# Which side of a PSUM-to-SBUF copy takes the step: writes in ascending order and interleaved reads, in place of the reverse

## The chip, the cores and the metric

The kernel runs on one core of one Trainium2 chip. The metric is the device time of one execution in microseconds (us), as the chip reports it. Before the change it was 951.44 us, the median of three runs (950.08 to 952.41).

## The reference

Attention within windows of 64 rows: q, k and v are fp32 of shape (4, 4096, 1536), and each window looks only at itself.

```python
q_w = q.reshape(B, nw, W, D)           # W = 64, nw = 64; k and v likewise
logits = np.einsum('bnwd,bnud->bnwu', q_w, k_w) * D ** -0.5
logits = logits - logits.max(axis=-1, keepdims=True)
attn = np.exp(logits)
attn = attn / attn.sum(axis=-1, keepdims=True)
out = np.einsum('bnwu,bnud->bnwd', attn, v_w)
```

## The kernel before

The 16384 rows are cut into 32 units of 512 rows. For each unit the kernel loads q, k and v from HBM (casting to fp16 on the way), transposes q and k on TensorE, multiplies, takes the exponential, multiplies with v, scales and stores. The transposes move pairs of fp16 as if they were fp32 words. Four transposes of 128x128 go into one of two PSUM buffers of 128x512 fp32, called banks here, and one copy then takes the bank to SBUF, alternately by VectorE (even g) and by ScalarE (odd g), 12 copies a unit. The cut below is shortened, with comments added.

```python
tps = [ps(f"tp{i}", [P, R, H, P]) for i in range(2)]     # two PSUM banks, R = H = 2
...
        for g in range(2 * DC):                  # TensorE; DC = 6; g < DC is q, then k
            transpose(g)                         # waits for the copy of g - 2 (same bank)
            if g >= DC + 2:
                for h in range(H):
                    product(g - DC - 2, h)
...
    def copy_out(eng, copy, g):
        xt = xq if g < DC else xk
        await_(eng, p_t[g % 2])                  # the four transposes of g are done
        if g % DC == DC - 1:
            eng.sem_inc(m_q if g < DC else m_k, 1)   # q16 or k16 may be loaded again
        dst = xt[:, g % DC, :].rearrange("p (r e j) -> p r j e", r=R, j=H)
        copy(out=dst, in_=tps[g % 2][:, :, :, :]).then_inc(f_c[g % 4], 1)
...
        gp.wait_ge(m_q, u + 1)                   # GpSimd issues the transfers
        load("q", u + 1, q16, d_q)
        ...
        gp.wait_ge(m_k, u + 1)
        load("k", u + 1, k16, d_k)
```

DC is 1536 / 256 = 6. The bank holds `r j e`; the products want `r e j` in SBUF. So somewhere the order has to turn. Before, the copy reads PSUM straight through and writes every second fp32 word of SBUF, a step of 8 bytes, then comes back for the words between.

The softmax here doesn't subtract the row's maximum and nothing guards it: scores larger than these inputs give would overflow.

## Time and profile before

| what | before |
|---|---|
| median time | 951.44 us |
| span of the profiled run | 949.5 us |
| bytes over HBM | 302 MB read, 101 MB written |
| busy: PE / VectorE / ScalarE | 609.7 / 278.7 / 331.3 us |
| the changed copies: VectorE / ScalarE | 192 of 692 ns / 192 of 617 ns |
| mean granted TensorE clock (1 is full speed) | 0.855 |

The page has one digit for each fortieth of the span (9 is 90% or more busy) and a list of groups of instructions: line, engine, operation, tiles, count, then the busy us in total, the mean ns of one, and the idle time of that engine in front of them. The lines themselves stand in the prediction. One view more, the list of waits: here is what TensorE's transposes waited for in the kernel before (engine, tile, line, what was waited for, us in total, times, longest us).

```profile
PE tp L148 <- PEq L214: 244.1, 33, 16.7
PE tp L148 <- DVE xq L223: 47.9, 64, 1.0
```

The first line is TensorE standing idle until q or k has been loaded; nearly all of it is the wait for k (224.9 us before the k transposes), 7 to 8 us in most units. The second is TensorE waiting for a copy to free a bank.

### The profile page before, as it was taken

The page shows a single profiled execution, that of the slowest core. Times are in us where ns is not written, and L with a number is a line of the kernel's source. Part 1 is how long each engine was busy: PE and PEld are TensorE (multiplying, and loading weights), DVE is VectorE, ACT ScalarE, POOL GpSimd, SP SyncE. Part 2 cuts the span into 40 slices and gives each one's busy share as a digit, 9 for nine tenths or more (in the row PEclk, how much of TensorE's full clock was granted, in tenths as well). Part 3 has the DMA queues.
Part 4 walks back from the last instruction along what each step waited for, and adds up shares of the span by engine and source line. Part 5 has one row for each costly group of instructions (what it writes and reads, how often), then busy time and mean ns, then how long its engine had stood idle before and what let it go on. Part 6 is the DMA issues. An engine that isn't in the chain of part 4 may idle for free. (4 is left out here: it accounts for less than half of the span.)

```text
span 949.5 us, 11240 instructions
## 1 busy us (share of the span) xinstructions
PE 609.7 (64%) x4096; PEld 393.6 (41%) x3456; DVE 278.7 (29%) x454; ACT 331.3 (35%) x642; POOL 97.4 (10%) x140
## 2 busy tenths in 40 slices
PE   2776855577565776656865558655577565776682
PEld 2544543354433444424544335443344433444450
DVE  1331413332133331333322333223332132331341
ACT  1442513443233432234432344323443233432252
POOL 4230100110001100101001010010110001100010
PEclk9997977997788987889887898787997788987796
DMA  9999999999999999999999999999999999999997
GB/s 249 216 284 283 238 247 282 279 284 267 235 277 281 285 280 238 261 280 283 283 254 245 281 280 284 272 234 272 281 283 281 243 256 281 282 282 261 235 236 300
DMA packets 26938, 253.34 MB, mean 267 GB/s; under 512 B 2096, under 2 KB 2096, under 8 KB 10544
## 3 DMA queue, kind: packets, MB, share of 16 engines
q0 software_dynamic: 26352, 248.52, 99.8%
q1 hardware_dynamic: 576, 4.72, 1.3%
q14 instruction: 8, 0.07, 0.0%
q8 instruction: 2, 0.03, 0.0%
HBM read 301.99 MB, written 100.66 MB: 424 GB/s over the span
## 5 line engine op out<-in xcount | busy, mean ns | idle before, releaser
L148 PE MATMUL tp<-ident,k 128*128 128x128 f32 x768 | 155.1, 349 | 231.4 <-PEq L214 224.9
L148 PEld LDWEIGHTS tp<-ident,k 128*128 128x128 f32 x768 | 120.4, 182 | 252.1 <-issue 249.6
L160 PE MATMUL lt<-xq,xk 128*128 128x256 f16 x1536 | 216.1, 293 | 0.0
L223 ACT COPY xk<-tp 128x512 f32<-128x512 f32 x96 | 59.2, 617 | 417.8 <-ACTq L214 417.8
L223 DVE COPY xk<-tp 128x512 f32<-128x512 f32 x96 | 66.5, 692 | 381.8 <-DVEq L214 381.8
L160 PEld LDWEIGHTS lt<-xq,xk 128*128 128x128 f16 x1536 | 160.1, 104 | 33.2
L148 PE MATMUL tp<-ident,q 128*128 128x128 f32 x768 | 104.0, 280 | 66.6 <-DVE xq L223 47.1
L148 PEld LDWEIGHTS tp<-ident,q 128*128 128x128 f32 x768 | 86.4, 143 | 100.5 <-issue 99.9
L269 ACT ACTIVATE et<-lt,zeros 32x128 f16<-32x128 f32 x256 | 92.0, 360 | 39.4 <-ACTq L214 36.2
L223 ACT COPY xq<-tp 128x512 f32<-128x512 f32 x96 | 59.3, 617 | 107.3 <-ACTq L214 107.3
L116 PE MATMUL o<-v,et 128*128 128x512 f16 x384 | 93.3, 379 | 0.0
L189 PEld LDWEIGHTS <-et 128*128 128x128 f16 x384 | 30.2, 97 | 151.3 <-issue 114.3
L256 DVE TENSOR_SCALAR out<-o,rs 128x512 f32<-128x512 f32 x128 | 90.2, 747 | 7.7
L223 DVE COPY xq<-tp 128x512 f32<-128x512 f32 x96 | 66.1, 689 | 78.0 <-DVEq L214 78.0
L116 PE MATMUL tp<-v,et 128*128 128x512 f16 x256 | 75.8, 377 | 0.0
L109 POOL DMA_DIRECT2D k<-in_k_dram x31 | 17.4, 562 | 416.5 <-ACTq L221 416.3
L246 DVE RECIPROCAL rs<-sp 128x2 f32<-128x2 f32 x64 | 10.6, 166 | 157.8 <-DVEq L214 157.6
L280 ACT ACTIVATE out<-tp,rs 128x512 f32<-128x512 f32 x64 | 44.0, 688 | 35.8 <-ACTq L214 31.3
L256 DVE TENSOR_SCALAR out<-tp,rs 128x512 f32<-128x512 f32 x64 | 48.1, 751 | 26.2 <-DVEq L214 26.2
L116 PE MATMUL lt<-v,et 128*128 128x512 f16 x128 | 48.3, 377 | 0.0
L109 POOL DMA_DIRECT2D v<-in_v_dram x29 | 20.5, 706 | 238.2 <-DVEq L255 238.2
L280 ACT ACTIVATE out<-o,rs 128x512 f32<-128x512 f32 x64 | 44.1, 688 | 0.0
(26 smaller groups left out, 132.6 us busy)
## 6 DMA issues: line engine op xcount, KB each, us to landing
out_dram<-out POOLq DMA_DIRECT2D x31, 3072.0 KB, 28.5
k<-in_k_dram POOLq DMA_DIRECT2D x31, 1536.0 KB, 20.6
q<-in_q_dram POOLq DMA_DIRECT2D x30, 1536.0 KB, 21.6
v<-in_v_dram POOLq DMA_DIRECT2D x29, 1536.0 KB, 18.9
vs<-in_v_dram POOLq DMA_DIRECT2D x2, 1536.0 KB, 29.7
out<-in_q_dram SPq DMA_DIRECT2D x2, 768.0 KB, 6.5
out<-in_q_dram SPq DMA_DIRECT2D x1, 1536.0 KB, 11.5
out<-in_q_dram POOLq DMA_DIRECT2D x1, 1536.0 KB, 22.7
```

The costliest lines, as they stand in the source:

```text
L109: nc.gpsimd.dma_start(out=slots(dst, 0, SLOTS, r), in_=rows(src, u * UR, SLOTS, r)).then_inc(s, 16)
L116: return nc.tensor.add_instruction(mybir.InstMatmult(name=nc.get_next_instruction_name(), engine=PE, ins=[low(rhs), low(w)], outs=[low(o)] ...
L148: ins = nc.tensor.transpose(tps[g % 2][:, r, j, :], pairs[:, c * P : (c + 1) * P], ident[:, :])
L160: ins = nc.tensor.matmul(lts[h][:, r, :, :], lhsT=halves(xk, c)[:, r, h, :, w], rhs=halves(xq, c)[:, :, h, :, w], start=(c == 0 and w == 0 ...
L189: ld = nc.tensor.ldweights(w)
L223: copy(out=dst, in_=tps[g % 2][:, :, :, :]).then_inc(f_c[g % 4], 1)
L246: ve.reciprocal(out=rs[:, n : n + R], in_=sp[:, n : n + R]).then_inc(n_d, 1)
L256: ins = ve.tensor_scalar_mul(scaled(u, n, j), bank(n, j), scalar1=rs[:, n : n + 1])
L269: ins = sc.activation(ets[h][s, :, :, s], lts[h][s, :, :, s], EXP, bias=zeros[s, 0:1], scale=scale)
L280: ins = sc.activation(scaled(u, n, j), bank(n, j), COPY, bias=0.0, scale=rs[:, n : n + 1])
```

## The change

Its intent is to let SBUF be written in ascending order, and to take the turn on the PSUM side: the copy alternates between two places of the bank that lie 512 bytes apart. The same words end up in the same places, and the instructions stay the same in number and order.

```diff
-        dst = xt[:, g % DC, :].rearrange("p (r e j) -> p r j e", r=R, j=H)
-        copy(out=dst, in_=tps[g % 2][:, :, :, :]).then_inc(f_c[g % 4], 1)
+        dst = xt[:, g % DC, :].rearrange("p (r e j) -> p r e j", r=R, j=H)
+        src = tps[g % 2][:, :, :, :].rearrange("p r j e -> p r e j")
+        copy(out=dst, in_=src).then_inc(f_c[g % 4], 1)
```

## The prediction

> **What bounds the kernel now.** I read the page's slices first, then the DMA queues, then the groups, the order of time on the GpSimd queue in mid-run, and last the ending.
>
> The slices show, for each fortieth of the span, busy tenths of an engine.
>
> ```profile
> PE   2776855577565776656865558655577565776682
> DVE  1331413332133331333322333223332132331341
> ACT  1442513443233432234432344323443233432252
> DMA  9999999999999999999999999999999999999997
> q0 software_dynamic: 26352, 248.52, 99.8%
> HBM read 301.99 MB, written 100.66 MB: 424 GB/s over the span
> ```
>
> The DMA row is full from the first slice to the last but one; VectorE and ScalarE are rarely above four tenths. The last line is the bytes that have to move whatever the engines do: 402.65 MB. [...]I take the kernel as DMA bound, and ask only whether the change can open a hole in that full row.
>
> The copies that the change touches are these four groups (line, engine, operation, tiles, count, busy us, mean ns, then the idle time before them). The fifth line is a PSUM reader with unit steps on both sides, as a yardstick.
>
> ```profile
> L223 ACT COPY xk<-tp 128x512 f32<-128x512 f32 x96 | 59.2, 617 | 417.8 <-ACTq L214 417.8
> L223 DVE COPY xk<-tp 128x512 f32<-128x512 f32 x96 | 66.5, 692 | 381.8 <-DVEq L214 381.8
> L223 ACT COPY xq<-tp 128x512 f32<-128x512 f32 x96 | 59.3, 617 | 107.3 <-ACTq L214 107.3
> L223 DVE COPY xq<-tp 128x512 f32<-128x512 f32 x96 | 66.1, 689 | 78.0 <-DVEq L214 78.0
> L256 DVE TENSOR_SCALAR out<-o,rs 128x512 f32<-128x512 f32 x128 | 90.2, 747 | 7.7
> ```
>
> They take 66.1 + 66.5 = 132.6 us of VectorE and 118.5 us of ScalarE, and those engines stand idle in front of them for 459.8 and 525.1 us. That idle time is the room for a slower copy.
>
> The timeline of the GpSimd queue gives when each transfer is issued (start us, us, what, idle before and releaser). First two units in which the data was late, then one in which it was not.
>
> ```profile
> 499.79 0.70 POOL L109 DMA_DIRECT2D v<-in_v_dram  x1 [8.51 <-DVEq L255]
> 504.30 0.56 POOL L109 DMA_DIRECT2D q<-in_q_dram  x1 [3.81 <-ACTq L221]
> 504.86 0.71 POOL L286 DMA_DIRECT2D out_dram<-out  x1
> 520.75 0.56 POOL L109 DMA_DIRECT2D k<-in_k_dram  x1 [15.18 <-ACTq L221]
> 529.82 0.71 POOL L109 DMA_DIRECT2D v<-in_v_dram  x1 [8.51 <-DVEq L255]
> ...
> 87.27 0.56 POOL L109 DMA_DIRECT2D k<-in_k_dram  x1 [17.34 <-ACTq L221]
> ...
> 107.90 0.56 POOL L109 DMA_DIRECT2D k<-in_k_dram  x1 [5.78 <-ACTq L221]
> ```
>
> From v to v is 30.0 us. A unit moves 402.65 / 32 = 12.6 MB, which in that time is 419 GB/s; the mean unit, (886.2 - 100.9) / 27 = 29.1 us between q issues, moves 433 GB/s. The unit from 87.27 to 107.90 is 20.6 us: there k already lay in place, and that is the pace of the compute alone. **So each unit has 29.1 - 20.6 = 8.5 us of slack on the compute side.**
>
> There is a second cushion, the queue itself. The k load issued at 520.75 finds the store of 504.86 in front of it, which takes 28.5 us (the median to landing) and so lands at 533.4: the engines have work for 12.6 us more. A k load could be issued up to some 10 us later without an idle engine.
>
> The ending has no cushion of that sort, so I read it apart (windows: busy us of PE, weight loads, VectorE, ScalarE, GpSimd, then clock, DMA share, GB/s).
>
> ```profile
> 930.00:935.00 5.00, 1.75 (x9) 0.20 (x2) 2.43 (x5) 1.84 (x3) 0.57 (x1) 0.88 1.01 430
> 935.00:940.00 5.00, 0.00 (x0) 0.00 (x0) 0.00 (x0) 0.00 (x0) 0.00 (x0) 0.50 1.01 433
> 940.00:945.00 5.00, 0.00 (x0) 0.00 (x0) 0.00 (x0) 0.00 (x0) 0.00 (x0) 0.50 0.46 197
> ```
>
> The engines finish at 932.9 and the DMA goes on to about 940 + 0.46 x 5 = 942.3. Only stores are left there. The first half of the last store is issued at 931.89; the DMA then has 942.3 - 931.9 = 10.4 us of work, of which the last store's own 3.15 MB takes 7.3 us at 430 GB/s. So 3.1 us of older stores still stand in front of it.
>
> [...]
>
> **The change part by part.** It adds and removes no instruction: the order on every engine is the same, the 384 copies stay, and matmuls read the same layout. No semaphore moves. What changes is the step on either side of the copies.
>
> 1. *Writing SBUF in order.* Nothing is gained[...]: 0 ns a copy.
> 2. *Reading PSUM interleaved.* Either free (692 and 617 ns stay)[...].
> 3. *On the path of one unit*, in the costly case. q transposes run in pairs with one copy on each engine, and each pair's transposes wait for the copies of the pair before (47.1 us in total of PE waiting for VectorE's xq copies). Two such waits lie in the q stage[...]. In the k stage the copies lie beside products; about one wait is exposed[...], and one more where k follows q at once. [...]against 8.5 us of slack: 0 us of the span in units 1 to 30.
> 4. *The start.* Four loads and the stores queue behind each other by then; the first refill, of q, is issued at 44.5, and the loads issued up to 17.5 are 6 x 7.3 = 44 us of work from 7.6 on, so till about 52. A delay of 2 to 3 us fits: 0 us.
> 5. *The ending.* From the k transposes of unit 30 (893.5) there is no more waiting for data except the last v, so the delays add up[...].
>
> Sum: 951.4 + 0 if the read is free[...].
>
> **The rivals.** (a) *The copies get faster and the time with them.* [...]A copy 100 ns faster would give at most 18 x 0.1 = 1.8 us in the ending, and that only if the stores in front were not the bound: 950 to 951. (b) [...]. (c) *The copies are slower, as in step 2, and a release comes so late that DMA idles.* For it: m_k and m_q are given by ScalarE in the order of its copies, so they do move. Against it: 12.6 us of queue in front of k. It would show less than a full DMA row.[...]
>
> **Range and chances.** [...]the middle is 952. The three runs of before spread over 2.3 us,[...] 949.5 to 954.5 for 8 times in 10. More than 2% slower needs 970, which only rival (b) reaches: 2%. More than 2% faster needs 932[...]: under 1%. The rest is within 2%.
>
> **What would show it.** Right: the DMA row still nines, HBM rate 423 to 425 GB/s, the wait of k's issue near 15 us less 1 to 2. Step 1 is wrong if a copy falls below 680 (VectorE) or 605 ns (ScalarE). Step 2 is read off the same four rows: unchanged[...]. Step 3 is wrong if the wait of PE for VectorE's xq copies in total grows by more than 32 x 1.5 us, step 5 if the last store is issued later than 936. The prediction as a whole is wrong if slices with a DMA share under nine appear in mid-run.

The sum came to 951.4 us if the read is free and to 952.9 us if it is not; the 952 lies between. Rival (b): a read so dear that the copies become the bound, at 985 us. An estimate: (b) needs each of the six pairs of a unit to take over 8.5 / 6 = 1.4 us longer before the slack is used up.

## The result, and the profile after

The changed kernel took 952.55 us (median of 4 runs, 952.39 to 952.75) against 951.65 us for the kernel before (4 runs, 950.08 to 952.41). The ratio is 1.0012 with a 95% interval of 0.9994 to 1.0029: the same.

The page of the changed kernel, in the lines that answer to those of before:

```profile
PE   2775755686565776666765567655587565776582
DVE  1331413332233321333322333223332132331341
ACT  1432513443233432244332344223343233432252
DMA  9999999999999999999999999999999999999996
HBM read 301.99 MB, written 100.66 MB: 424 GB/s over the span
...
L224 ACT COPY xk<-tp 128x512 f32<-128x512 f32 x96 | 56.3, 586 | 417.3 <-ACTq L214 417.3
L224 DVE COPY xk<-tp 128x512 f32<-128x512 f32 x96 | 66.4, 692 | 378.8 <-DVEq L214 378.8
L224 ACT COPY xq<-tp 128x512 f32<-128x512 f32 x96 | 56.3, 586 | 113.6 <-ACTq L214 113.6
L224 DVE COPY xq<-tp 128x512 f32<-128x512 f32 x96 | 66.1, 688 | 81.8 <-DVEq L214 81.8
```

The row of DMA is as full as before and HBM runs at the same 424 GB/s. VectorE's copies are what they were (688 to 692 ns). ScalarE's copies are 586 ns in place of 617, and the spread is gone: they ran from 608 to 635 ns before and from 586 to 587 after. So 192 x 31 ns = 6.0 us of ScalarE's work have vanished, and nothing came of it. The unit in mid-run shows why (timeline of the GpSimd queue: start us, us, transfer, idle before and releaser):

```profile
500.58 0.71 POOL L109 DMA_DIRECT2D v<-in_v_dram  x1 [8.51 <-DVEq L256]
...
521.51 0.56 POOL L109 DMA_DIRECT2D k<-in_k_dram  x1 [15.14 <-ACTq L221]
530.57 0.71 POOL L109 DMA_DIRECT2D v<-in_v_dram  x1 [8.51 <-DVEq L256]
```

From v to v is 30.0 us again. In front of k's issue the queue waits 15.14 us in place of 15.18: the transfers set the pace, as before. In the ending, the stretch of time from unit 30's k transposes to the last store's issue was 932.91 - 893.57 = 39.3 us before and is 933.69 - 894.58 = 39.1 us.

### The profile page after: what moved, and what is told of

It is laid out like the page before. It is cut to its first block, busy times and chain, and to the rows that moved or that the text cites. A ratio compares the mean times of both kernels' runs of the same rounds, so it can differ in the third digit from the quotient of the medians.

```text
span 950.7 us, 11240 instructions
## 1 busy us (share of the span) xinstructions
PE 611.6 (64%) x4096; PEld 395.1 (42%) x3456; DVE 278.7 (29%) x454; ACT 325.3 (34%) x642; POOL 97.3 (10%) x140
## 5 line engine op out<-in xcount | busy, mean ns | idle before, releaser
L148 PE MATMUL tp<-ident,k 128*128 128x128 f32 x768 | 155.2, 349 | 227.7 <-PEq L214 220.7
L160 PE MATMUL lt<-xq,xk 128*128 128x256 f16 x1536 | 216.5, 293 | 0.0
L224 ACT COPY xk<-tp 128x512 f32<-128x512 f32 x96 | 56.3, 586 | 417.3 <-ACTq L214 417.3
L148 PE MATMUL tp<-ident,q 128*128 128x128 f32 x768 | 105.5, 282 | 69.1 <-DVE xq L224 46.5
L224 ACT COPY xq<-tp 128x512 f32<-128x512 f32 x96 | 56.3, 586 | 113.6 <-ACTq L214 113.6
L109 POOL DMA_DIRECT2D v<-in_v_dram x29 | 20.4, 705 | 238.2 <-DVEq L256 238.2
```

Of the source, the lines that this page charges most:

```text
L109: nc.gpsimd.dma_start(out=slots(dst, 0, SLOTS, r), in_=rows(src, u * UR, SLOTS, r)).then_inc(s, 16)
L148: ins = nc.tensor.transpose(tps[g % 2][:, r, j, :], pairs[:, c * P : (c + 1) * P], ident[:, :])
L160: ins = nc.tensor.matmul(lts[h][:, r, :, :], lhsT=halves(xk, c)[:, r, h, :, w], rhs=halves(xq, c)[:, :, h, :, w], start=(c == 0 and w == 0 ...
L224: copy(out=dst, in_=src).then_inc(f_c[g % 4], 1)
```

## The experiments

Two questions were open. What does each side of a copy cost, in itself? And is there really no time to be had or lost by a copy in this kernel, or did a gain and a loss cancel? The first four runs answer the first question. The diffs below are shortened: `# q:` and `# k:` stand for the two branches of `if g < DC`, and `.then_inc(...)` is left out where it did not change.

**e_sides: both sides straight, and both sides stepped.** In q copies neither side has a step, in k copies both have. The data comes out scrambled, so the result is wrong.

```diff
+        line = xt[:, g % DC, :]
+        bank_ = tps[g % 2][:, :, :, :].rearrange("p r j e -> p (r j e)")
+        # q:
+        copy(out=line, in_=bank_)
+        # k:
+        copy(out=line.rearrange("p (m j a) -> p a m j", j=2, a=2),
+             in_=bank_.rearrange("p (j a m) -> p a m j", j=2, a=2))
```

> Wrong results on purpose. q copies have unit steps on both sides; k copies have the stepped write of before (8 bytes) and an interleaved read together. Theory (the interleaved read is free, the stepped write costs ScalarE 31 ns): q copies 586 ns on ScalarE and 692 on VectorE, k copies 617 and 692. Rival (the read is what made ScalarE faster, or unit steps on both sides would be faster still): q copies below 570 on ScalarE or below 680 on VectorE, or k copies 586. Time within 0.5% of before.

Groups of copies, with their mean ns after the busy us:

```profile
L227 ACT COPY xk<-tp 128x512 f32<-128x512 f32 x96 | 59.5, 619 | 418.8 <-ACTq L214 418.8
L225 ACT COPY xq<-tp 128x512 f32<-128x512 f32 x96 | 56.3, 586 | 107.7 <-ACTq L214 107.7
L227 DVE COPY xk<-tp 128x512 f32<-128x512 f32 x96 | 66.5, 693 | 382.0 <-DVEq L214 382.0
L225 DVE COPY xq<-tp 128x512 f32<-128x512 f32 x96 | 66.1, 688 | 76.4 <-DVEq L214 76.4
```

A copy with no step at all (586 and 688 ns) is no faster on either engine than the changed one (586, and 688 to 692), so the interleaved read of PSUM cost nothing here. The stepped write alone brings ScalarE's 31 ns (617 before, 619 here), whether or not the read has a step too. The rival falls.

**e_write: longer steps of the write.** Reads are straight; q copies write one word of each 16 bytes; k copies put successive words 512 bytes apart, going round four places. Its output is wrong, which doesn't matter for the time.

```diff
+        # q:
+        copy(out=line.rearrange("p (m a) -> p a m", a=4), in_=bank_.rearrange("p (a m) -> p a m", a=4))
+        # k:
+        copy(out=line.rearrange("p (a m) -> p m a", a=4), in_=bank_.rearrange("p (m a) -> p m a", a=4))
```

> Wrong results on purpose. Reads have unit steps; q copies write with a step of 16 bytes[...], k copies with a step of 512 bytes. Theory[...]: longer than at 8 bytes on ScalarE[...], and on VectorE above 692 for the first time[...]. Rival (the 31 ns are the price of any pattern with a step, whatever its size): 617 on ScalarE and 692 on VectorE for both.

```profile
L225 ACT COPY xq<-tp 128x512 f32<-128x512 f32 x96 | 102.0, 1062 | 109.8 <-ACTq L214 109.8
L227 ACT COPY xk<-tp 128x512 f32<-128x512 f32 x96 | 101.6, 1058 | 339.2 <-ACTq L214 339.2
L225 DVE COPY xq<-tp 128x512 f32<-128x512 f32 x96 | 101.2, 1054 | 80.6 <-DVEq L214 80.6
L227 DVE COPY xk<-tp 128x512 f32<-128x512 f32 x96 | 100.7, 1049 | 316.6 <-DVEq L214 316.6
```

A step of 16 bytes costs VectorE 1054 - 688 = 366 ns and ScalarE 1062 - 586 = 476 ns, and 512 bytes cost no more than 16. So of the two distances the longer one did not count. Why such writes take longer was not shown, and no step between 8 and 16 bytes was tried. A step of 8 bytes cost nothing on VectorE (692 ns either way) and 31 ns on ScalarE. The rival, the same price for any step, falls. And with copies half as long again or more, the single run, of unknown state, took 951.61 us, much as the kernel before.

**e_read: longer steps of the read.** The changed read goes back and forth between only two places; a longer round might have cost more. Here q copies read with a step of 16 bytes, k copies go round four places 512 bytes apart. Writes are straight. Its output is wrong, which doesn't matter for the time.

```diff
+        # q:
+        copy(out=line.rearrange("p (a m) -> p a m", a=4), in_=bank_.rearrange("p (m a) -> p a m", a=4))
+        # k:
+        copy(out=line.rearrange("p (m a) -> p m a", a=4), in_=bank_.rearrange("p (a m) -> p m a", a=4))
```

> Wrong results on purpose. Writes have unit steps; q copies read PSUM with a step of 16 bytes, k copies round robin over four places 512 bytes apart. The changed kernel's read alternates between two places only[...]. Theory (a read of PSUM by these engines costs the same in any order): 586 ns on ScalarE and 692 on VectorE for both. Rival[...]: the 16-byte step or the four places, or both, show more[...].

```profile
L227 DVE COPY xk<-tp 128x512 f32<-128x512 f32 x96 | 66.4, 692 | 380.4 <-DVEq L214 380.4
L227 ACT COPY xk<-tp 128x512 f32<-128x512 f32 x96 | 56.3, 587 | 419.1 <-ACTq L214 419.1
L225 ACT COPY xq<-tp 128x512 f32<-128x512 f32 x96 | 56.3, 586 | 110.3 <-ACTq L214 110.3
```

VectorE's q copies were 688. In all the patterns tried, straight, between two places, with a step of 16 bytes and round four places, the copies took 688 to 692 ns on VectorE and 586 to 587 on ScalarE.

**e_split: fixed cost or rate.** Every copy is done in two halves of 256 columns, q in the form of before, k in the form of after. The result is right.

```diff
+        for r in range(R):
+            ins = copy(out=..., in_=...)       # the half r, in the one form or the other
+        ins.then_inc(f_c[g % 4], 1)
```

> Right results. Every copy is done in two halves of 256 columns, q with the stepped write of before, k with the interleaved read of after. It tells whether ScalarE's 31 ns are a fixed cost of an instruction or a rate. Theory (a rate: 0.06 ns for each element written with a step): [...]16 apart. Rival (fixed): halves 31 apart[...].[...]

```profile
L226 ACT COPY xq<-tp 128x256 f32<-128x256 f32 x192 | 64.0, 389 | 110.2 <-ACTq L214 110.2
L232 ACT COPY xk<-tp 128x256 f32<-128x256 f32 x192 | 62.1, 375 | 408.6 <-ACTq L214 408.6
```

The halves are 14 ns apart, close to half of 31: ScalarE's cost went with the number of words written, 31 / 512 = some 0.06 ns each. With the copies of 512 there are now two lengths for each form. With the step, (617 - 389) / 256 = 0.89 ns a word over a fixed 161 ns; without it, (586 - 375) / 256 = 0.82 ns a word over a fixed 164. VectorE's halves took 419 and 420 ns, (688 - 419) / 256 and (692 - 420) / 256 = 1.05 to 1.06 ns a word, so much the same in both forms.

**t_null and t_after: is the 0.9 us between the medians real?** The first result left a difference of 0.1%. The kernel before and the changed one were both timed again, five rounds, on one chip, with no edit.

> The kernel before, unaltered, timed against itself: it shows how small a difference these rounds can tell. Theory (the 0.9 us between the medians of after and before are scatter of the transfers): ratio 1.000 with an interval of about 0.2% either way, and single runs that spread over 2 us as before. Rival (the kernel before is steady and after is really 1 us slower): runs of this kernel stay within 0.5 us of each other around 951.4.

> The changed kernel, unaltered, in the same rounds as the null. Theory: ratio 0.999 to 1.002, with one among the intervals covering 1; copies 692 ns on VectorE and 586 on ScalarE again. Rival (the change costs about 1 us, by some way yet to be found): ratio 1.001 with an interval that excludes 1, in rounds in which the null includes it.

The null gave 951.53 us (950.96 to 952.78), ratio 0.9998, interval 0.9985 to 1.0012. The changed kernel gave 951.91 us (950.66 to 953.59), ratio 1.0001, interval 0.9988 to 1.0015; the kernel before in these rounds had 951.91 us (9 runs). The 0.9 us did not come back, and an effect of more than about 0.15% either way is excluded. That is all that can be said: a tenth of a microsecond could not be seen here.

**e_eight: longer copies, in pieces.** Each copy of the changed kernel is cut in eight pieces of 64 elements, which needs no added semaphore. A copy then takes 1.14 us on VectorE and 1.03 on ScalarE in the timeline, against 0.69 and 0.59. The result is right.

```diff
-        copy(out=dst, in_=src).then_inc(f_c[g % 4], 1)
+        for r in range(R):
+            for e in range(0, P, P // 4):
+                ins = copy(out=dst[:, r, e : e + P // 4, :], in_=src[:, r, e : e + P // 4, :])
+        ins.then_inc(f_c[g % 4], 1)
```

> Right results. The changed kernel with every copy in eight pieces of 64 elements[...]. Theory (8.5 us of compute slack in each unit, and a backlog of stores at the end): the time grows by 0 to 2 us, 951 to 954. Rival (slower copies delay the releases, and DMA idles): [...]1010 or more.

It took 952.58 us (4 runs, 951.95 to 953.34) against 951.59 us; ratio 1.0008, interval 0.9991 to 1.0025. The theory holds, the rival of 1010 us falls. The waits of TensorE in this run show where the longer copies went:

```profile
PE tp L148 <- PEq L214: 178.1, 29, 16.7
PE tp L148 <- DVE xq L226: 80.3, 68, 1.5
PE tp L148 <- DVE xk L226: 19.7, 32, 1.0
```

The wait for loaded data shrank from 242.9 us in the changed kernel to 178.1, by 65 us or 2.1 us a unit. The waits for copies grew from 49.6 to 100.3 us, by 51 us or 1.6 us a unit; the busy time of TensorE's groups grew as well, by 21 us (q transposes 105.5 to 119.9, k transposes 155.2 to 156.9, products 216.5 to 221.5), at a mean clock of 0.819 in place of 0.857. Slack was turned into waiting for copies and into slower matmuls, and the transfers noticed nothing. Only in the ending is there no slack: from unit 30's k transposes to the last store's issue took 936.74 - 894.85 = 41.9 us, 2.8 more than in the changed kernel. The windows show that the backlog of stores then just ran out (five us each; the last two numbers are DMA share and GB/s):

```profile
935.00:940.00 5.00, 0.58 (x3) 0.00 (x0) 1.61 (x3) 1.30 (x3) 0.57 (x1) 0.79 0.90 375
940.00:945.00 5.00, 0.00 (x0) 0.00 (x0) 0.00 (x0) 0.00 (x0) 0.00 (x0) 0.50 0.86 361
```

The share of 0.90 is a hole of half a microsecond. In the changed kernel the second of these windows has a share of 0.64, so the transfers ended about (0.86 - 0.64) x 5 = 1.1 us later here: of the 2.8 us, 1.1 showed.

**e_thirtytwo: copies long enough to use up the slack.** The same with 32 pieces of 16 elements (`P // 16` in place of `P // 4`). The result is right.

> Right results. The changed kernel with every copy in 32 pieces of 16 elements[...]. Theory: the unit's compute grows[...] from 20.6 to about 32, which is more than the 29.1 of its transfers: the slack is used up and the time is 1000 to 1070. Rival (the slack is larger than I read it): under 970.

It took 1141.98 us, ratio 1.1998 (1.1978 to 1.2018). A copy took 260.3 / 96 = 2.7 us on VectorE and 244.5 / 96 = 2.5 on ScalarE (busy time of the q copies). Copies do become the bound, so the slack is finite, as the theory has it. But the size is missed: from its third k issue at 108.05 to its last at 1086.25 a unit takes 978.2 / 28 = 34.9 us, not 32. The next runs say where the rest is.

**l_before, l_after, l_eight, l_thirtytwo: the same kernels with little to transfer.** The loads of units 3 to 30 and all stores but the last two move half of their bytes (223 MB in all), so that the compute is what remains. The results are wrong. The edit is the same in all four; l_eight and l_thirtytwo have the pieces as well.

```diff
+        if 3 <= u < N - 1:                     # in load; in store: if u < N - 2
+            o, i = o[:, :, : r * D // 2], i[:, :, : r * D // 2]
         nc.gpsimd.dma_start(out=o, in_=i).then_inc(s, 16)
```

> Wrong results on purpose. The kernel before with half the bytes in the loads of units 3 to 30 and in all but the last two stores: 223 MB in place of 402.65, some 515 us of transfers. Theory (DMA is the bound before, and the compute alone needs 20.6 us a unit): the time falls to about 28 x 20.6 + 87 + 40 = 700, 690 to 720. Rival (the engines' chain is nearly as long as the transfers): over 850.

> Wrong results on purpose. The same lightening of the changed kernel; with l_before it shows what the change is worth where the compute is the bound. Theory (VectorE's copy, which did not change, paces the transposes; ScalarE's 31 ns end beside other work): within 0.3% of l_before. Rival (ScalarE's copies are on the path): shorter by 3 to 6 us, that is 32 units with 3 to 6 copies of 31 ns.

> Wrong results on purpose. The same lightening with every copy in eight pieces. It measures without the transfers what slower copies add to a unit. Theory (my sum of a unit: four waits of PE for a copy[...]): 2.1 us a unit, about 65 us more than l_after. Rival (the copies lie beside products and only the q stage counts): about 1 us a unit, 32 us.

> Wrong results on purpose. The same lightening with every copy in 32 pieces. Theory: about 11 us a unit more than l_after, some 1050; and if the compute is then the bound in both, e_thirtytwo with its full transfers comes within 3% of it. Rival: this kernel stays well under e_thirtytwo, so that transfers and compute add up in place of overlapping.

| kernel | median us (runs) | ratio to the kernel before | us between k issues | clock of the profiled run |
|---|---|---|---|---|
| l_before | 697.60 (4) | 0.7335 | 20.4 | 0.985 |
| l_after | 697.71 (4) | 0.7337 | 20.4 | 0.985 |
| l_eight | 798.03 (4) | 0.8397 | 23.8 | 0.879 |
| l_thirtytwo | 1136.08 (1) | - | 34.7 | 0.765 |

The us between issues are the last k issue less the third, over 28 units. Half of the bytes gone brings the time to 698 us, as expected, so the transfers were the bound, and the 20.4 us a unit confirm the 20.6 that the prediction read from one unit. With the compute as the bound, the medians of before and after are still 0.1 us apart (696.31 to 698.49 and 697.39 to 697.90): ScalarE's 31 ns lie beside other work. In l_after TensorE's transposes wait 63.7 + 16.8 = 80.5 us for VectorE's copies, which did not change, and the list of waits names no copy of ScalarE. The rival, a gain of 3 to 6 us, falls.

And l_thirtytwo, a single run of unknown state, comes within 0.6% of e_thirtytwo: at that length of copy the full transfers cost next to nothing more. Its own 1136 us missed the expected 1050. Against l_after TensorE's waits for copies grew by 298 us, or 9.3 us a unit, less than the 11 expected; but the busy time of its groups grew by 154 us too (657.0 to 811.4 in the sum of the list), 4.8 us a unit, at a mean clock of 0.765.

l_eight missed its expectation of 65 us: it is 100 us above l_after. The groups of TensorE's transposes say where the rest is. First l_after, then l_eight:

```profile
L149 PE MATMUL tp<-ident,k 128*128 128x128 f32 x768 | 114.2, 279 | 41.7 <-DVE xk L225 16.8 <-DVE xq L225 16.2 <-PEq L215 8.6
L149 PE MATMUL tp<-ident,q 128*128 128x128 f32 x768 | 103.9, 279 | 67.0 <-DVE xq L225 47.5 <-PEq L215 19.2
```

```profile
L149 PE MATMUL tp<-ident,k 128*128 128x128 f32 x768 | 148.7, 339 | 47.1 <-DVE xk L227 21.3 <-DVE xq L227 20.9 <-PEq L215 4.9
L149 PE MATMUL tp<-ident,q 128*128 128x128 f32 x768 | 123.7, 314 | 93.8 <-DVE xq L227 77.4 <-PEq L215 16.4
```

The same transposes take 314 to 339 ns in place of 279. TensorE's idle time before its groups grew from 132.9 to 166.0 us, by 33 us, and the span from 695.6 to 792.7, by 97 us; the other 64 us are busy time. So a third of the loss is idle time, and two thirds are slower matmuls, at a mean clock of 0.879 in place of 0.985. The waits for copies alone grew from 80.5 to 119.9 us, by 39 us: 30 of them in front of the q transposes and 9 in front of the k transposes. That is near the rival's 32 us from the q stage alone, and not the theory's 65; neither had the clock.

The mean clock is 0.86 from 500 to 548 us of l_eight and 1.00 from 500 to 541 us of l_after. The timeline of e_eight, with the same pieces, has one unit in detail: eight q transposes at 500.42 take 1.04 us, the next eight 1.06 after a wait of 1.45 us for a copy, and the eight after those 1.94 after another wait of 1.00. In the kernel before the three take 1.04, 1.06 and 1.06 us, with waits of 1.00 and 0.55. That the longer waits lowered the clock is a reading of these traces; no run held the clock fixed.

## Why the prediction was right

The measured 952.55 us lies in the range of 949.5 to 954.5 and 0.6 us from the predicted 952; in the later rounds the changed kernel had 951.91 us. Point by point:

- **What bounds the kernel** was right. The DMA row is still full, and taking away bytes (l_before) takes 253 us off the time, while copies 65 to 75% longer (e_eight) do not move it. At the 433 GB/s of the mean unit and of the window 935 to 940, the 402.65 MB take 930 us, an estimate.
- **Step 1, "0 ns a copy" for writing SBUF in order,** was right on VectorE and wrong on ScalarE, by the test that the prediction itself set (a copy below 605 ns). It measured 31 ns. The working behind the 0 split ScalarE's 617 ns into a share for the words, from no trace, and a remainder that I took as fixed, without a second copy of other length or form to compare; e_sides and e_split show that 31 of the 617 were the stepped write, and go with the words written: 0.89 ns a word with the step, 0.82 without, over 161 to 164 fixed. The spread of ScalarE's copies, 608 to 635 ns, which the trace of before had already shown, was the hint that I passed over.
- **Step 2, the price of the interleaved read,** was left at even chances. It cost nothing: e_sides and e_read settle it (586 to 587 and 688 to 692 ns in every pattern). So the 1.5 us between the two sums were not there. That the middle still fell so close is partly luck: the median of the kernel before itself lay at 950.78 to 951.91 us from one set of rounds to the next.
- **Step 3, four longer waits in a unit for the costly case,** did not arise. What longer copies cost a unit, e_eight shows with pieces: 65 us less slack in 31 units is 2.1 us. The step counted waits alone, and these grew by 1.6 us a unit; the rest is mostly slower matmuls. With few transfers (l_eight) the waits for copies grew by only 1.2 us a unit, mostly in the q stage, and yet the same pieces cost 3.4 us a unit in all; the step had too much waiting in the k stage and lacked the slower clock (0.879 in place of 0.985).
- **Step 4, nothing at the start,** is supported by e_eight's time (ratio 1.0008).
- **Step 5, a longer ending, of which a part shows,** did not arise either; its figures came from no trace. With e_eight's longer copies the ending grew by 2.8 us, of which 1.1 showed at the end of the transfers. The mean time grew by 0.8 us, which the interval cannot tell from nothing.
- **The rivals.** (a), faster copies, came in part: 31 ns on ScalarE, and no time from it even where compute is the bound (l_after). (b), copies that become the bound, did not come from the change, and e_thirtytwo shows that it would start somewhere between 1.1 and 2.7 us a copy, at a higher price than was reckoned. (c), late releases that idle DMA, is refuted at 1.1 us a copy.

## What to carry to other kernels

When the DMA row is full, price a change by the cushion in front of it: the engine's wait for its data, and the queue's backlog; then prove the cushion by making the cost larger on purpose. Where a copy from PSUM has to reorder fp32 words, put the turn on the reading side: here it was free in every pattern tried (586 to 587 ns on ScalarE, 688 to 692 on VectorE), while a write with a step of 16 or 512 bytes made a copy 52 to 81% longer (1049 to 1062 ns). In this kernel the change of side gained no time. And do not call a remainder fixed until two lengths have been compared.
